# A float32 matmul with leaky ReLU: the transposes of A on VectorE as 32-bit elements, with stationary operands interleaved by two

One core of one Trainium2 chip. The metric is the time on the device in microseconds (us), the median of several executions; lower is better.

## The reference

```python
def setup_inputs():
    m, k, n = 4096, 4096, 4096
    return {"a": randn(m, k) float32, "b": randn(k, n) float32, "alpha": 0.01}     # shortened

def reference(a, b, alpha):
    x = np.matmul(a, b)
    return np.where(x > 0, x, alpha * x)
```

## The kernel before

The kernel rounds both inputs to bf16 while it loads them and keeps TensorE busy with 8192 matmuls of 128x128 by 128x512. It hands A to its matmuls with k on the partitions, so A has to be transposed. The first block (512 rows by 1024 in k) goes through TensorE itself ("turned"); all the others are loaded by GpSimd's queue into `a16` and transposed by VectorE in 32x32 squares, 62 instructions in all, each for 256 rows and 1024 in k.

```python
KC, NT, MT, NP = 8, 512, 4, 2           # KC: neighbours in k that share a partition
...
at[mb, h, u] = at_pool.tile([P, KC, RM], BF16, name="at")          # stationary operands

def load_a(mb, h, u, mp):
    dst = new_a(mb, h, u)[:, :, 2 * mp * P:2 * (mp + 1) * P]
    ...                                                             # 4 loads into a16
    nc.vector.transpose(
        dst.rearrange("p c (g i) -> p g c i", g=8), a16.rearrange("p g (j c) -> p g c j", c=KC)
    )

def mm(ps, mb, h, pi, u, mt, nt, c, first, last):
    nc.tensor.matmul(ps, at[mb, h, u][:, c, mt * P:(mt + 1) * P],
                     bt[pi, u][:, c, nt * NT:(nt + 1) * NT], start=first, stop=last)

def quarter_of(pieces, quarter):        # spreads the loads of a later step over this one
    for piece in pieces[len(pieces) * quarter // 4:len(pieces) * (quarter + 1) // 4]:
        piece()

# the first rows and columns go in eight steps of 64 matmuls; a step that ends a turn adds its
# PSUM banks into SBUF, one of four blocks of rows at a time:
for quarter in range(4):
    ...                                 # 16 matmuls
    if last:
        spill(t, h, quarter, banks)     # two VectorE adds
    quarter_of(following, quarter)      # loads and transposes for the step after
```

With two pieces, `quarter_of` places them at the end of the second and of the fourth quarter of a step, so the last transpose for the next step stands behind the last adds of this one. And inside a 32x32 square the transpose reads elements that lie KC = 8 bf16 values, 16 bytes, apart.

Of the kernel before, what the change touches and what calls it, by code (L numbers as in the profile page):

```python
# [8 lines left out]
P = 128  # L9
BF16 = mybir.dt.bfloat16  # L10
FP32 = mybir.dt.float32
LRELU = mybir.ActivationFunctionType.Lrelu
KC = 8
NT = 512
# [9 lines left out]
def kernel(  # L24
# [4 lines left out]
    alpha,  # L29
    out: bass.AP,  # L30
):



# [8 lines left out]
    nc = tc.nc  # L43
# [7 lines left out]
    RM = MT * P  # L51
# [8 lines left out]
    at_pool = ctx.enter_context(tc.tile_pool(name="at", bufs=HALVES * KU))  # L60
# [12 lines left out]
    w = small_pool.tile([P, NT], BF16, name="w")  # L73
    nc.vector.memset(w, 0.0)  # L74
    x = small_pool.tile([P, 8], FP32, name="x")
    nc.vector.memset(x, 0.0)  # L76
    nc.scalar.activation(x, x, LRELU, alpha=alpha)  # L77
    wp = psum_pool.tile([P, NT], FP32, name="ps")
    for _ in range(8):
        nc.tensor.matmul(wp, w[:, :P], w, start=True, stop=True)  # L80

    at = {}
    bt = {}

    def new_a(mb, h, u):
        if (mb, h, u) not in at:
            at[mb, h, u] = at_pool.tile([P, KC, RM], BF16, name="at")
        return at[mb, h, u]

    def new_b(pi, u):  # L90
# [3 lines left out]

    def load_a(mb, h, u, mp):

        dst = new_a(mb, h, u)[:, :, 2 * mp * P:2 * (mp + 1) * P]
        row = (mb * HALVES + h) * RM + 2 * mp * P
        a16 = a16_pool.tile([P, 8, QW], BF16, name="a16")
        for q in range(4):  # L100
            src = a[row:row + 2 * P, u * KW + q * QW:u * KW + (q + 1) * QW]
            nc.gpsimd.dma_start(a16[32 * q:32 * q + 32], src.rearrange("(g i) w -> i g w", i=32))  # L102
        nc.vector.transpose(  # L103
            dst.rearrange("p c (g i) -> p g c i", g=8), a16.rearrange("p g (j c) -> p g c j", c=KC)
        )

    def b_rows(n, u, c):
# [7 lines left out]
    def mm(ps, mb, h, pi, u, mt, nt, c, first, last):  # L115
        nc.tensor.matmul(  # L116
            ps,
            at[mb, h, u][:, c, mt * P:(mt + 1) * P],
            bt[pi, u][:, c, nt * NT:(nt + 1) * NT],
            start=first,  # L120
            stop=last,
        )

    def new_banks():
        return {
            (mt, nt): psum_pool.tile([P, NT], FP32, name="ps")
            for mt in range(MT)
# [3 lines left out]
    def place(mb, h, n, mt):  # L131
        row = ((mb * HALVES + h) * MT + mt) * P
        return out[row:row + P, n * RN:(n + 1) * RN]
# [20 lines left out]
    for mb in range(1, MB):  # L154
        first = next(i for i, r in enumerate(regions) if r[0] == mb)
        for h in range(HALVES):
            for u in range(KU):
                loads.setdefault(first * KU + h * KU + u - 2 * KU + 1, []).extend(
                    lambda mb=mb, h=h, u=u, mp=mp: load_a(mb, h, u, mp) for mp in range(MT // 2)
                )  # L160
# [13 lines left out]
    def step_loads(h, u):  # L174
        if h:
            return [lambda mp=mp: load_a(0, 1, u, mp) for mp in range(MT // 2)]
        made = [lambda c=c: load_b(0, pairs[0], u, c) for c in range(KC)]
        made.insert(4, lambda: load_a(0, 0, u, 1))
        made.insert(0, lambda: load_a(0, 0, u, 0))
        return made  # L180
# [4 lines left out]
    def spill(t, h, mt, banks):  # L185
# [10 lines left out]
        if t == len(TURNS) - 1:  # L196
            o = o_pool.tile([P, RN], FP32, name="o")
            nc.scalar.activation(o, part[h][:, mt, :], LRELU, alpha=alpha)  # L198
            nc.scalar.dma_start(place(0, h, pairs[0], mt), o)


    a_in = bt_pool.tile([P, MT, KW], FP32, name="a_in", tag="bt")
    b_in = [part_pool.tile([P, KC // 2, RN], FP32, name="b_in", tag="part") for _ in range(2)]
    a_rounded = at_pool.tile([P, MT, KW], BF16, name="a_rounded", tag="at")
    order = [("a", 0), ("b", 0), ("a", 1), ("b", 1), ("b", 2), ("a", 2), ("b", 3), ("a", 3),
             ("b", 4), ("b", 5), ("b", 6), ("b", 7)]
    for what, i in order:
        if what == "a":
            nc.sync.dma_start(a_in[:, i, :], a[i * P:(i + 1) * P, :KW])  # L209
        else:  # L210
            nc.sync.dma_start(b_in[i // 4][:, i % 4, :], b_rows(pairs[0], 0, i))  # L211
    a0 = new_a(0, 0, 0)
    b0 = new_b(0, 0)
    turned = {
        (mt, i): psum_pool.tile([P, KC // 2, P], BF16, name="turned", tag="ps")
        for mt in range(MT)
        for i in range(2)
    }
    banks = new_banks()

    def take(what, i):
        if what == "b":
            nc.scalar.copy(b0[:, i, :], b_in[i // 4][:, i % 4, :])  # L223
            return
        nc.vector.tensor_copy(a_rounded[:, i, :], a_in[:, i, :])  # L225
        cols = a_rounded[:, i, :].rearrange("m (p c) -> m c p", c=KC)
        for c in range(KC):
            nc.tensor.transpose(turned[i, c // 4][:, c % 4, :], cols[:, c, :], ident)  # L228
        nc.scalar.copy(a0[:, :4, i * P:(i + 1) * P], turned[i, 0])  # L229
        nc.vector.tensor_copy(a0[:, 4:, i * P:(i + 1) * P], turned[i, 1])  # L230

    there = {"a": [], "b": []}
    ready = []
# [1 line left out]
    for n, (what, i) in enumerate(order):  # L235
        take(what, i)
        if (what, i) == ("b", 3):

            nc.gpsimd.tensor_copy(x[:, :1], b0[:, 2, :1])  # L239
        there[what].append(i)  # L240
        now = [(i, c) for c in there["b"]] if what == "a" else [(mt, i) for mt in there["a"]]
        ready.append(now)
        for mt, c in ready[n - 1] if n else []:
            for nt in range(NP):
                mm(banks[mt, nt], 0, 0, 0, 0, mt, nt, c, (mt, nt) not in begun, False)
                begun.add((mt, nt))
# [3 lines left out]
    for mt, c in ready[-1]:  # L250
        for nt in range(NP):
            mm(banks[mt, nt], 0, 0, 0, 0, mt, nt, c, False, True)
        spill(0, 0, mt, banks)
# [3 lines left out]
    for i in range(1, len(steps)):  # L257
        t, h, u, first, last = steps[i]
        following = queue[i + 1] if 2 <= i and i + 1 < len(steps) else []
        own = 2 * KU - 2 + i - (len(steps) - 2)  # L260
        if first:
            banks = new_banks()
            if h not in part:
                part[h] = part_pool.tile([P, MT, RN], FP32, name="part", tag="part")
        for quarter in range(4):
            if last:
                todo = [(quarter, c) for c in range(KC)]
            else:
                todo = [(mt, c) for c in (2 * quarter, 2 * quarter + 1) for mt in range(MT)]
            for mt, c in todo:  # L270
                for nt in range(NP):
                    mm(banks[mt, nt], 0, h, 0, u, mt, nt, c, first and c == 0,
                       last and c == KC - 1)
            if last:
                spill(t, h, quarter, banks)
            quarter_of(following, quarter)
            if own >= 2 * KU - 2:
                quarter_of(loads.get(own, []), quarter)


    for r in range(HALVES, len(regions)):
        mb, h, pi, n = regions[r]
        banks = new_banks()
        final = r == len(regions) - 1
        for u in range(KU):
            last = u == KU - 1
            for mt in range(MT):
# [7 lines left out]
                if last:  # L295
                    o = o_pool.tile([P, RN], FP32, name="o")
                    to = place(mb, h, n, mt)
                    for nt in range(NP):
                        cols = slice(nt * NT, (nt + 1) * NT)
                        nc.scalar.activation(o[:, cols], banks[mt, nt], LRELU, alpha=alpha)  # L300
                        if final:
# [39 lines left out]
```

## Time and profile before

| kernel before | value | where from |
|---|---|---|
| time | 1795.21 us (1794.66 to 1795.24) | three executions |
| pace of matmuls | 215.8 ns | chain of waits, after 110 us |
| gaps of TensorE after 20 us | 6.36 us, four | waits |
| half clock after the largest gap | about 6.8 us | windows |
| one transpose on VectorE | 3842 ns | groups |
| VectorE busy | 264.3 us | page, part 1 |

In the lines PE is TensorE, PEld its weight loads, DVE VectorE, ACT ScalarE and POOL GpSimd; L103 is line 103 of the kernel. The granted clock is the share of its full clock that TensorE got, so half clock is 0.50. A group's line ends with the idle time of the engine just before it and with what ended that. TensorE's ends are modelled, so pace is read from starts. In a line of the windows the columns are: stretch, its length, busy us (and instructions) of TensorE, of its weight loads, of VectorE, ScalarE and GpSimd, then granted clock, busy share of the DMA engines and GB/s. The prediction shows the lines themselves.

### The profile page before, as it was taken

The numbers are of one execution on the slowest core, as the hardware profiler recorded it, in microseconds if no ns is written. First come the engines' busy times: TensorE is split into PE (matmuls) and PEld (weight loads), VectorE is DVE, ScalarE is ACT, GpSimd is POOL, SyncE is SP. The second block draws the span as 40 slices with busy tenths as digits, with TensorE's granted clock in tenths as the row PEclk, the third lists the DMA queues.
The fourth block names the chain that finished last, engine by engine and source line by source line (L and its number), as shares of the span: only waits on it lengthen the run. The fifth ranks groups of instructions, "written<-read, shape, count | busy, mean of one in ns | idle before, by whom it ended". The sixth has DMA issues, their size and how long they took to land.

```text
span 1794.5 us, 17965 instructions
## 1 busy us (share of the span) xinstructions
PE 1771.5 (99%) x8068; PEld 806.3 (45%) x8232; DVE 264.3 (15%) x112; ACT 155.1 (9%) x270; POOL 360.7 (20%) x663
## 2 busy tenths in 40 slices
PE   8999999999999999999999999999999999999999
PEld 4434444444444444444444444444444444444444
DVE  5750000055300000005520000000551000000000
ACT  3010000000000000000000000000000000000001
POOL 4530110333002021033300202004320120201000
PEclk9999999999999999999999999999999999999999
DMA  9993571987319256298713916539770481835511
GB/s 253 195 239 86 122 160 47 182 127 123 85 58 194 55 118 141 63 200 124 122 56 88 192 48 117 119 94 197 125 124 24 101 180 48 157 78 117 118 47 47
DMA packets 147020, 214.06 MB, mean 119 GB/s; under 512 B 12800, under 2 KB 76288, under 8 KB 146944
## 3 DMA queue, kind: packets, MB, share of 16 engines
q0 software_dynamic: 126208, 139.50, 48.1%
q10 hardware_dynamic: 17856, 65.02, 9.3%
q1 hardware_dynamic: 2880, 8.39, 1.2%
q8 instruction: 64, 1.05, 0.2%
q14 instruction: 12, 0.10, 0.0%
HBM read 285.21 MB, written 67.11 MB: 196 GB/s over the span
## 4 chain that ended last, share of the span: by engine, by line
PE 97%; DMA 2%; issue 1%; DVE 0%; ACT 0%; POOL 0%; SPq 0%; DVEq 0%; POOLq 0%
PE ps L116 97%; DMA a<-in_a_dram 1%; DMA a_in<-in_a_dram 0%; DVE at L103 0%; DVE part L195 0%; PE turned L228 0%; ACT part L193 0%; POOL a L102 0%; DVE a_rounded L225 0%; ACT o L300 0%; SPq L211 0%; SPq L209 0%; DVEq L195 0%; POOLq L102 0%
## 5 line engine op out<-in xcount | busy, mean ns | idle before, releaser
L116 PE MATMUL ps<-bt,at 128*128 128x512 bf16 x8028 | 1765.0, 380 | 14.9 <-DVE at L103 5.5
L116 PEld LDWEIGHTS <-at 128*128 128x128 bf16 x8192 | 802.3, 98 | 976.1 <-DVE at L103 7.4
L113 POOL DMA_DIRECT2D bt<-in_b_dram x408 | 217.3, 539 | 1097.4 <-PE ps L116 908.0
L103 DVE STREAM_TRANSPOSE at<-a 128x2048 bf16<-128x2048 bf16 x62 | 235.6, 3842 | 1046.0 <-PE ps L116 1033.7
L300 ACT ACTIVATE o<-ps 128x512 f32<-128x512 f32 x240 | 130.7, 595 | 1524.6 <-PE ps L116 1462.5
L102 POOL DMA_DIRECT2D a<-in_a_dram x248 | 142.3, 579 | 201.3 <-DVE at L103 142.8
L195 DVE TENSOR_TENSOR part<-ps,part 128x512 f32<-128x512 f32 x32 | 20.3, 680 | 33.7 <-PE ps L116 31.6
L198 ACT ACTIVATE o<-part 128x1024 f32<-128x1024 f32 x8 | 8.5, 1057 | 86.0 <-DVE part L195 79.2
L223 ACT CAST bt<-b_in 128x1024 bf16<-128x1024 f32 x8 | 8.1, 1045 | 2.2 <-DMA b_in<-in_b_dram 2.0
L228 PE MATMUL turned<-ident,a_rounded 128*128 128x128 bf16 x32 | 3.6, 276 | 3.3 <-DVE a_rounded L225 3.3
L193 ACT COPY part<-ps 128x512 f32<-128x512 f32 x8 | 4.4, 594 | 14.2 <-PE ps L116 14.2
L228 PEld LDWEIGHTS <-a_rounded 128*128 128x128 bf16 x32 | 3.1, 156 | 5.2 <-DVE a_rounded L225 4.7
L191 DVE COPY part<-ps 128x512 f32<-128x512 f32 x8 | 5.2, 838 | 0.0
L80 PE MATMUL ps<-w 128*128 128x512 bf16 x8 | 3.6, 631 | 1.2 <-DVE x L76 1.2
L225 DVE CAST a_rounded<-a_in 128x1024 bf16<-128x1024 f32 x4 | 2.8, 693 | 6.5 <-DMA a_in<-in_a_dram 6.5
L229 ACT COPY at<-turned 128x512 bf16<-128x512 bf16 x4 | 2.3, 585 | 8.6 <-PE turned L228 8.6
L239 POOL CAST x<-bt 128x1 f32<-128x1 bf16 x1 | 0.6, 558 | 11.1 <-ACT bt L223 11.1
L230 DVE COPY at<-turned 128x512 bf16<-128x512 bf16 x4 | 1.7, 424 | 5.2 <-PE turned L228 5.2
L80 PEld LDWEIGHTS <-w 128*128 128x128 bf16 x8 | 1.0, 142 | 2.8 <-issue 1.6
L77 ACT ACT_TABLE_LOAD x1 | 1.3, 1283 | 0.7 <-PEq L322 0.7
L74 DVE MEMSET w<- 128x256 uint32 x1 | 0.3, 272 | 0.9 <-PEq L322 0.9
masks.py:199 POOL TENSOR_SCALAR_AFFINE_SELECT ident<-ident 128x128 bf16<-128x128 bf16 x1 | 0.3, 287 | 0.1
(7 smaller groups left out, 0.9 us busy)
## 6 DMA issues: line engine op xcount, KB each, us to landing
bt<-in_b_dram POOLq DMA_DIRECT2D x408, 256.0 KB, 7.6
out_dram<-o ACTq DMA_DIRECT2D x124, 512.0 KB, 3.8
a<-in_a_dram POOLq DMA_DIRECT2D x248, 128.0 KB, 5.0
b_in<-in_b_dram SPq DMA_DIRECT2D x8, 512.0 KB, 9.6
a_in<-in_a_dram SPq DMA_DIRECT2D x4, 512.0 KB, 7.8
out_dram<-o SPq DMA_DIRECT2D x8, 256.0 KB, 2.0
```

The source lines that it names most:

```text
L80: nc.tensor.matmul(wp, w[:, :P], w, start=True, stop=True)
L102: nc.gpsimd.dma_start(a16[32 * q:32 * q + 32], src.rearrange("(g i) w -> i g w", i=32))
L103: nc.vector.transpose(dst.rearrange("p c (g i) -> p g c i", g=8), a16.rearrange("p g (j c) -> p g c j", c=KC))
L113: nc.gpsimd.dma_start(new_b(pi, u)[:, c, :], b_rows(n, u, c))
L116: nc.tensor.matmul(ps, at[mb, h, u][:, c, mt * P:(mt + 1) * P], bt[pi, u][:, c, nt * NT:(nt + 1) * NT], start=first, stop=last,)
L191: nc.vector.tensor_copy(kept, banks[mt, nt])
L193: nc.scalar.copy(kept, banks[mt, nt])
L195: nc.vector.tensor_add(kept, banks[mt, nt], kept)
L198: nc.scalar.activation(o, part[h][:, mt, :], LRELU, alpha=alpha)
L223: nc.scalar.copy(b0[:, i, :], b_in[i // 4][:, i % 4, :])
L228: nc.tensor.transpose(turned[i, c // 4][:, c % 4, :], cols[:, c, :], ident)
L300: nc.scalar.activation(o[:, cols], banks[mt, nt], LRELU, alpha=alpha)
```

## The change

VectorE is to transpose half as many elements: two bf16 neighbours in k count as one 32-bit element. A square of 32x32 such elements then carries two columns of k at once, so the stationary operands of two neighbours lie interleaved, and TensorE reads its 128 columns 4 bytes apart.

```diff
-at[mb, h, u] = at_pool.tile([P, KC, RM], BF16, name="at")
+at[mb, h, u] = at_pool.tile([P, KC // 2, RM, 2], BF16, name="at")
...
         nc.vector.transpose(
-            dst.rearrange("p c (g i) -> p g c i", g=8), a16.rearrange("p g (j c) -> p g c j", c=KC)
+            dst.rearrange("p c m e -> p c (m e)").bitcast(U32).rearrange("p c (g i) -> p g c i", g=8),
+            a16.rearrange("p g w -> p (g w)").bitcast(U32)
+            .rearrange("p (g j c) -> p g c j", g=8, c=KC // 2),
         )
...
-            at[mb, h, u][:, c, mt * P:(mt + 1) * P],
+            at[mb, h, u][:, c // 2, mt * P:(mt + 1) * P, c % 2],
...
-        nc.scalar.copy(a0[:, :4, i * P:(i + 1) * P], turned[i, 0])
-        nc.vector.tensor_copy(a0[:, 4:, i * P:(i + 1) * P], turned[i, 1])
+        for half, copy in ((0, nc.scalar.copy), (1, nc.vector.tensor_copy)):
+            copy(
+                a0[:, 2 * half:2 * half + 2, i * P:(i + 1) * P, :].rearrange("p c m e -> p c e m"),
+                turned[i, half].rearrange("p (c e) m -> p c e m", e=2),
+            )
```

The read step stays 16 bytes: four 32-bit elements in place of eight of 16 bits.

## The prediction

> **What bounds the kernel now.** I read the page first, for the engine that fills the span.

> ```profile
> span 1794.5 us, 17965 instructions
> PE 1771.5 (99%) x8068; PEld 806.3 (45%) x8232; DVE 264.3 (15%) x112; ACT 155.1 (9%) x270; POOL 360.7 (20%) x663
> L116 PE MATMUL ps<-bt,at 128*128 128x512 bf16 x8028 | 1765.0, 380 | 14.9 <-DVE at L103 5.5
> L116 PEld LDWEIGHTS <-at 128*128 128x128 bf16 x8192 | 802.3, 98 | 976.1 <-DVE at L103 7.4
> L103 DVE STREAM_TRANSPOSE at<-a 128x2048 bf16<-128x2048 bf16 x62 | 235.6, 3842 | 1046.0 <-PE ps L116 1033.7
> L230 DVE COPY at<-turned 128x512 bf16<-128x512 bf16 x4 | 1.7, 424 | 5.2 <-PE turned L228 5.2
> ```

> TensorE is busy all the time; VectorE, whose work the change halves, is busy for 15% of it. A matmul's 380 ns is a modelled, overlapping duration. The pace is in the chain in order of time: its pieces of 49 recorded matmuls start 10.79 us apart, which is 50 matmuls (2% of the records, 164 of 8192, are missing) and 215.8 ns each. 8192 x 215.8 ns = 1767.8 us. So at most 1794.5 - 1767.8 = 26.7 us are not steady matmuls, and the change can gain from those alone. About 10 us of them pass before the first real matmul. The rest is in the waits and the TensorE timeline:

> ```profile
> DVE at L103 <- PE ps L116: 1033.7, 23, 337.7
> POOL a L102 <- DVE at L103: 142.8, 32, 7.8
> DVE at L103 <- DMA a<-in_a_dram: 6.0, 1, 6.0
> PE ps L116 <- DVE at L103: 5.5, 2, 4.0
> PE ps L116 <- ACT part L193: 0.6, 1, 0.6
> PE ps L116 <- DVE part L195: 0.2, 1, 0.2
> ```

> ```profile
> 27.39 42.48 PE L116 MATMUL ps<-bt,at 128*128 128x512 bf16 x193 [0.60 <-ACT part L193]
> 71.40 0.73 PE L116 MATMUL ps<-bt,at 128*128 128x512 bf16 x2 [1.54 <-DVE at L103]
> 72.35 27.14 PE L116 MATMUL ps<-bt,at 128*128 128x512 bf16 x123 [0.22 <-DVE part L195]
> 103.50 26.78 PE L116 MATMUL ps<-bt,at 128*128 128x512 bf16 x108 [4.00 <-DVE at L103]
> ```

> Four gaps, 6.36 us, all before 104 us. After 110 us TensorE waits for no other engine. There VectorE waits 1033.7 us for TensorE, and what waits for VectorE is the issue of loads needed much later. The chain charges 1.3% to loads of A; I don't believe it, since VectorE waited for such a load only once (6.0 us, before the first transpose). The largest gap, seen from VectorE, and what follows it, in windows (PE, weight loads, DVE, ACT, POOL, then the granted clock):

> ```profile
> 98.45 1.29 DVE L195 TENSOR_TENSOR part<-ps,part 128x512 f32<-128x512 f32 x2 [0.65 <-PE ps L116]
> 99.66 11.19 DVE L103 STREAM_TRANSPOSE at<-a 128x2048 bf16<-128x2048 bf16 x3
> 102.00:103.00 1.00, 0.00 (x0) 0.00 (x0) 1.00 (x1) 0.00 (x0) 0.38 (x1) 0.75 1.12 281
> 106.00:107.00 1.00, 1.00 (x4) 0.42 (x3) 1.00 (x1) 0.00 (x0) 0.23 (x1) 0.50 1.06 307
> 110.00:111.00 1.00, 1.00 (x6) 0.49 (x5) 0.84 (x1) 0.00 (x0) 0.24 (x2) 1.00 1.14 213
> ```

> The transpose of the second half of the next A block stands in program order behind the last add of the step before, so it cannot start until TensorE has ended that step. TensorE then does four matmuls and sits idle for the rest of the transpose. The clock drops to 0.50 at about 102.5, 3.0 us into the gap, and returns at about 109.2. In between weight loads start 427 ns apart: 5.7 us / 0.427 = 13.5 matmuls, each 211 ns late, 2.85 us more. The gap costs nearly 7 us, not 4.

> [...]

> **The change part by part.** No instruction is added or removed: each engine has as many, in the same order; only patterns and widths differ.

> *Transposes (62).* Each handles 1024 elements of four bytes in place of 2048 of two. Elements on the reading side still lie 16 bytes apart. A 32x32 block takes 3842/64 = 60 ns now[...]. If that stays per element, the new duration is half, 1.92 us; I take 1.95.[...] VectorE loses 62 x 1.89 = 117 us of busy time, 264 to about 147, and that by itself is worth nothing.

> *Gap at 103.50.* It ends with a transpose that starts at 99.74 and takes 3.71 us here; 1.9 us off leaves about 2.1 us: -1.9 us.[...] I give 3 in 4 that the clock stays up: -2.85 x 0.75 = -2.1 us.

> *Gaps at 71.40 and 72.35.* The transpose at 67.31 follows an add that ends when TensorE still has about 2.4 us of the step to go. With 1.95 us, also removing the lateness inherited from the transposes at 56.28 and 61.20, it ends near 68.7, before TensorE asks for it at about 69.7; the next add then starts sooner as well. Some 0.1 us may stay: -1.6 us.

> *Gap at 27.39.* ScalarE's copy and the first transpose (23.37 to about 27.2) end together. If the copy only came last by chance, 0.6 goes; if it rules, nothing: -0.3 us.

> *Start.* The four VectorE copies out of PSUM now write at a step of two elements[...]. ScalarE's four (585 ns)[...] stay. Only the copy ahead of the last cast of A stands close to TensorE's path (0.05 us of slack before the last transposes at 16.20): +0.3 us.

> *Weight loads (8192).* This is the one part on the path everywhere. Columns lie 4 bytes apart, not 2. The kernel contains a harsher test: the 32 loads of the first transposes step by 16 bytes. The last eight of them, with the clock up, took 142 to 152 ns against 98, and eight load-and-transpose pairs went by in 0.66 us. A 4-byte step should lie between: I expect 98 to 125 ns. Under a matmul's 215.8 ns even 150 stays hidden. 0 us.

> Sum: 1795.2 - 1.9 - 2.1 - 1.6 - 0.3 + 0.3 = 1789.6, say **1789.5 us**, a third of a per cent.

> **The rivals.** *A: strided weight loads slow the stream.* For: each is before its matmul, all 8192 count, and one nanosecond on the pace is 8.2 us, more than the whole gain. Against: 117 ns of slack and the 16-byte loads. If the pace took 4.5 ns more the kernel would be 2% slower, about 1830 us. I give any visible slowing 6%. *B: a four-byte transpose costs twice a two-byte one* (limited by bytes or by two passes). Then all gaps stay and the start costs 0.3: 1795.5 us.[...] 10%. *C: the transpose drops to 1.2 us* because single two-byte writes were the limit: 0.7 us more from the large gap, and the clock surely stays up: 1788 us. 25%. *D: the clock still falls* after a 2.1 us gap: 1791.7 us. *E: a load takes the place of the transpose.* Early on the DMA engines are always busy (9 in the first slices), and a faster VectorE could find A not there. Against: issues land in 7 us (median), and the loads for the critical transposes were issued over 15 us ahead; only the first transpose had to wait. It would keep 1 to 2 us of the gain.

> **Range and chances.** Removing every gap and the clock drop gives 1795.2 - 6.4 - 2.85 = 1786, the low end. The high end, 1795, covers B nearly, D and E. Beyond 2% faster there is nothing to win (26.7 us of 1794.5 is 1.5%); beyond 2% slower only A. Faster 0.01, same 0.96, slower 0.03.

> **What would show it.** Right: transposes near 1.95 us, VectorE busy near 147 us; the gap near 100 us at about 2 us with the clock at 1.00 after it; no gap over 0.4 us near 70;[...] weight loads under 150 ns and chain pieces still 10.79 us apart. Wrong: another spacing of those pieces (A), transposes at 3.8 us (B), a clock of 0.5 after the gap (D), or a TensorE or VectorE wait for a load of A near 70 or 100 us (E).

## The result

1789.38 us, the median of four executions (1787.44 to 1790.58), against 1794.93 us before. The ratio is 0.997, with a 95% interval of 0.9952 to 0.9987. It is a small gain, "same" at the 2% line. Five more executions beside the experiments gave 1787.88 us (1787.49 to 1790.3), ratio 0.9962. The changed kernel spreads over 3 us; why is part of what follows.

The page of the changed kernel, with the lines that answer to those shown of before:

```profile
span 1785.7 us, 18129 instructions
PE 1775.6 (99%) x8232; PEld 805.0 (45%) x8232; DVE 153.8 (9%) x112; ACT 155.5 (9%) x270; POOL 360.9 (20%) x663
L120 PE MATMUL ps<-bt,at 128*128 128x512 bf16 x8192 | 1769.8, 379 | 2.2 <-DVE at L105 2.2
L120 PEld LDWEIGHTS <-at 128*128 128x128 bf16 x8192 | 801.6, 98 | 969.1 <-DVE at L105 2.7
L105 DVE STREAM_TRANSPOSE at<-a 128x1024 uint32<-128x1024 uint32 x62 | 123.0, 2020 | 1136.0 <-PE ps L120 1123.6
L234 ACT COPY at<-turned 128x512 bf16<-128x512 bf16 x4 | 2.9, 730 | 7.2 <-PE turned L232 7.2
L234 DVE COPY at<-turned 128x512 bf16<-128x512 bf16 x4 | 2.9, 733 | 3.7 <-PE turned L232 3.7
```

The transpose fell from 3842 to 2020 ns. The weight loads, now at a 4-byte step, take 98 ns as before. The copies from PSUM at the start became slower on both engines, 733 ns for 424 on VectorE and 730 for 585 on ScalarE. TensorE waits 2.2 us for VectorE's transposes, and for nothing else, after the start. Its timeline has a single gap (the number in brackets is the idle time):

```profile
15.31 80.02 PE L120 MATMUL ps<-bt,at 128*128 128x512 bf16 x370
97.55 42.69 PE L120 MATMUL ps<-bt,at 128*128 128x512 bf16 x197 [2.22 <-DVE at L105]
```

Of the four gaps before, those at 27.39, 71.40 and 72.35 us are gone, and that of 4.00 us is 2.22 us. From the windows of the same run, one in the gap and one after it:

```profile
96.00:97.00 1.00, 0.00 (x0) 0.00 (x0) 1.00 (x1) 0.62 (x1) 0.54 (x1) 1.00 1.44 193
98.00:99.00 1.00, 1.00 (x6) 0.49 (x5) 1.00 (x1) 0.00 (x0) 0.80 (x2) 1.00 1.17 280
```

The last but two number is the granted clock: it stays at 1.00, where the kernel before had 0.50 after its gap. For the pace, the chain in order of time from 300 to 600 us, first a piece of the kernel before (one record in fifty is missing there), then the whole of it in the changed kernel:

```profile
306.44 10.74 PE ps L116 x49
317.24 10.74 PE ps L116 x49
```

```profile
299.96 300.22 PE ps L120 x1391
```

10.79 us for 50 matmuls and 300.22 us for 1391 are both 215.8 ns.

The two profiled spans differ by 8.8 us, and the parts add up to that: gaps 6.36 - 2.22 = 4.1 us; 0.5 us more for the three gaps that vanished, since each began at a modelled end, 0.16 us later than the pace (379 - 216 ns); half clock 2.85 us; and a start of the steady matmuls at 15.31 in place of 16.70 us, 1.4 us. The last item isn't credited to the change: this start differs from execution to execution (below). The profiled execution of the changed kernel was the fastest of its four, that of the kernel before, 1796.25 us, lay above all its four timed ones. Over many executions the gain is 5 to 7 us.

### The profile page after: what moved, and what is told of

It reads as the page before. It is cut to its first block, busy times and chain, and to the rows that moved or that the text cites. A ratio compares the mean times of both kernels' runs of the same rounds, so it can differ in the third digit from the quotient of the medians.

```text
span 1785.7 us, 18129 instructions
## 1 busy us (share of the span) xinstructions
PE 1775.6 (99%) x8232; PEld 805.0 (45%) x8232; DVE 153.8 (9%) x112; ACT 155.5 (9%) x270; POOL 360.9 (20%) x663
## 4 chain that ended last, share of the span: by engine, by line
PE 99%; DMA 0%; DVE 0%; SPq 0%; issue 0%; ACT 0%; DVEq 0%
PE ps L120 99%; DMA a_in<-in_a_dram 0%; DVE at L105 0%; SPq L215 0%; PE turned L232 0%; SPq L213 0%; DVE part L199 0%; DVE a_rounded L229 0%; ACT o L307 0%; DVEq L105 0%
## 5 line engine op out<-in xcount | busy, mean ns | idle before, releaser
L105 DVE STREAM_TRANSPOSE at<-a 128x1024 uint32<-128x1024 uint32 x62 | 123.0, 2020 | 1136.0 <-PE ps L120 1123.6
L195 DVE COPY part<-ps 128x512 f32<-128x512 f32 x8 | 5.0, 691 | 0.2 <-PE ps L120 0.2
```

Of the source, the lines that this page charges most:

```text
L105: nc.vector.transpose(dst.rearrange("p c m e -> p c (m e)").bitcast(U32).rearrange("p c (g i) -> p g c i", g=8), a16.rearrange("p g w -> p ...
L195: nc.vector.tensor_copy(kept, banks[mt, nt])
```

## The experiments

The theory: the gain is what a shorter transpose saves at a few places before 105 us, together with the clock, which fell to 0.50 with the gap of 4.00 us. The rivals: the layout or the start brings it; VectorE's time or traffic over the whole run counts; strided weight loads cost something; loads take the transposes' place. The line numbers differ between kernels; the names of the tiles don't.

### The changed kernel again

No edit.

> The changed kernel once more, for more samples and a second profile. Theory (the gain is the shorter transposes in the gaps before 105 us, and the clock that does not fall): about 5 to 6 us below the kernel before, the gap near 97 us at 2.2 us, no gap near 70 us. The first four timed runs lay 3.1 us apart, and the profiled one was the fastest and started its steady matmuls 1.4 us earlier than the kernel before. Rival (the clock falls in some executions after a 2.2 us gap): a run of 1790 us or more with a stretch at half clock after the gap. If the spread is only in the start, the clock stays at 1.00 after 20 us.

1787.88 us against 1795.19. The gap is again 2.22 us, yet in this execution the clock did fall:

```profile
98.00:99.00 1.00, 0.91 (x3) 0.36 (x4) 1.00 (x2) 0.00 (x0) 0.78 (x2) 0.71 1.16 209
100.00:101.00 1.00, 1.00 (x4) 0.38 (x3) 1.00 (x1) 0.00 (x0) 0.02 (x1) 0.50 1.07 307
102.00:103.00 1.00, 1.00 (x6) 0.44 (x5) 0.00 (x0) 0.00 (x0) 0.12 (x1) 1.00 1.07 303
```

The half clock lasted from about 98.4 to 101.8 us, 3.4 us, half as long as in the kernel before, and cost 1.7 us. So the prediction's rival D occurs in some executions. The profiles hold six gaps of 2.2 us (this one, the first profile's, and those of "first rows", "forms", the first try of the layout alone, and "every transpose twice" near 70 us, all below); the clock fell after three of them, this one and the last and "forms", each time for 3.4 us.

The falls of the clock explain part of the 3 us of spread. The start is another part: the steady matmuls began between 14.9 and 17.1 us over the profiles of all versions but that with the 16-byte step, and the later the half clock of the start ended (10.8 to 14.8 us in the ten traces of these that record its end), the later they began (correlation 0.90; which of the two is the cause was not tested). The gapless version below spreads over 1.8 us in ten executions.

### The transposes one quarter earlier

```diff
-for piece in pieces[len(pieces) * quarter // 4:len(pieces) * (quarter + 1) // 4]:
+for piece in pieces[(len(pieces) * quarter + 3) // 4:(len(pieces) * (quarter + 1) + 3) // 4]:
```

With two pieces this places them at the end of the first and third quarters. On the changed kernel:

> The changed kernel with the first rows' transposes of A one quarter of a step earlier in program order, so that the transpose no longer stands behind the last adds of a step. Theory: the 2.2 us gap goes, 2 us below the changed kernel, about 1787 us, and the clock never falls after the start. Rival (the gap is really the load of A landing late): the gap stays, now put down to a load.

1785.47 us (1785.26 to 1785.66), ratio 0.9944 to the kernel before; again on another chip, 1785.22 us, ratio 0.9947. What was expected there:

> The changed kernel with the earlier transposes, as the partner of the run above on the same chip, and to see on another day or chip that it holds: 1785 to 1786 us, no gap after 20 us.

TensorE's timeline has no gap at all:

```profile
15.73 124.48 PE L120 MATMUL ps<-bt,at 128*128 128x512 bf16 x576
```

In the first of these runs the spread fell to 0.4 us too. On the kernel before, with its two-byte transposes and plain layout:

> The kernel before (two-byte transposes, plain layout) with the same earlier place in program order. Theory: the 3.84 us transpose fits between the third block's adds and the end of the step, so the 4.0 us gap and the clock drop after it go (6.9 us) and part of the gaps near 70 us; about 1787 to 1789 us, as good as the changed kernel, with slow transposes. Rival (the width of the transposes itself is what counts, by less traffic or less VectorE time over the whole run): it stays near 1795 us.

1789.08 us (1788.49 to 1790.47), ratio 0.9966, with transposes of 3842 ns:

```profile
69.75 0.94 PE L116 MATMUL ps<-bt,at 128*128 128x512 bf16 x3 [0.65 <-DVE at L103]
70.92 27.14 PE L116 MATMUL ps<-bt,at 128*128 128x512 bf16 x125 [0.22 <-DVE part L195]
98.68 0.94 PE L116 MATMUL ps<-bt,at 128*128 128x512 bf16 x3 [0.62 <-DVE at L103]
99.84 40.52 PE L116 MATMUL ps<-bt,at 128*128 128x512 bf16 x187 [0.22 <-DVE part L195]
```

The gap of 4.00 us shrank to 0.62 + 0.22 us and the clock stayed up. One line of scheduling brings about as much as the whole change, and the two together more than either, since a long transpose still makes VectorE late by some 0.6 us near 70 and 98 us. What counts is when a transpose ends, not how wide its elements are.

### Four-byte transposes for the first rows only

```diff
+        if mb:
+            nc.vector.transpose(...)      # as in the kernel before, plain layout
+            return
```

> Four-byte transposes and the interleaved layout only for the first 1024 rows of A (14 of the 62 transposes); the other 48 as before. Theory: only those before 105 us are on the path, so the time equals that of the changed kernel within 1 us, and VectorE is busy about 48 x 1.82 = 87 us longer than there. Rival (VectorE's time over the whole run counts, or strided weight loads cost something later): it differs from the changed kernel by over 2 us.

1790.24 us (1788.02 to 1790.39), ratio 0.997 against the changed kernel's 0.9962 in the same rounds. The medians lie 2.4 us apart, more than I expected and by itself over the rival's 2 us, but the executions of both reach from about 1788 to 1790.4, and the medians mostly say where more of them fell; by the means (1789.6 and 1788.6) it is 1.0 us. The trace has the same single gap, 2.21 us, and the rest of the run is without any. VectorE is busy for 241.3 us against 153.6, 88 us more, and that cost TensorE no wait. The 48 later transposes are off the path.

### The layout alone, twice

The first try wrote the new layout by two two-byte transposes, for the even and then for the odd columns:

```diff
+        for e in range(2):                # second try: for e in (1, 0)
+            nc.vector.transpose(
+                dst[:, :, :, e].rearrange("p c (g i) -> p g c i", g=8), src16[:, :, :, e, :]
+            )
```

> The interleaved layout alone: two-byte transposes write it, in two instructions of 1024 elements each (even and odd columns). Theory: the pair takes about 3.9 us, all gaps and the clock drop are as in the kernel before, the pace of the matmuls stays 215.8 ns; 1795 us, plus up to 0.3 us at the start. Rival (the layout or its strided weight loads brings or costs time): differs from the kernel before by over 2 us.

1793.1 us (1790.04 to 1794.96), ratio 0.999 (0.9977 to 1.0002). Not what I had in mind: TensorE uses an even column first, so it went on after the first half, and the large gap in the trace was 2.23 us. The second try turned the order round:

> The interleaved layout alone once more, because the first try had a flaw: its two half transposes wrote the even columns first, which TensorE uses first, so the gap near 100 us was only 2.2 us. Here the odd columns come first, so that TensorE has to wait for both halves, about 4 us. Theory: gaps and clock drop as in the kernel before, pace 215.8 ns, time within 1.5 us of the kernel before. Rival (the layout itself brings the gain of the first try, 1.8 us or more): again 1793 us or less.

1795.48 us, ratio 1.0005 (0.9992 to 1.0017), with the gap back:

```profile
101.99 38.23 PE L120 MATMUL ps<-bt,at 128*128 128x512 bf16 x163 [4.11 <-DVE at L107]
```

The half clock is back as well (0.60 from 100 to 105 us), and the pace from 300 to 600 us is again 1391 matmuls in 300.22 us. The layout gains and costs nothing that can be measured. The first try shows in passing that splitting a transpose, so that what is needed first ends first, halves the gap too.

### Every transpose twice, and one of them twice

```diff
-        nc.vector.transpose(...)
+        for _ in range(2):                # the other: range(2 if (mb, h, u, mp) == (0, 1, 2, 1) else 1)
+            nc.vector.transpose(...)
```

> The changed kernel with every four-byte transpose done twice in a row, 2 x 2.02 us, so as long as the old one. Theory: the gain is undone, gap of 4.2 us near 97 to 100 us, half clock after it, gaps near 70 us back; 1794 to 1796 us. Rival (width or traffic counts, not the duration at that place): stays near 1789 us.

1797.34 us against 1794.87, ratio 1.0011 (0.9998 to 1.0025). The gain is undone (whether more than that is lost is within the interval): gaps of 0.27 us near 26, 2.24 us near 70 and 4.23 us near 104 us, and here the clock fell after both of the long ones.

> The changed kernel with one single transpose of 62 done twice: the one that stands in the 2.2 us gap. Theory: the gap grows by 2.0 us to 4.2 us, the clock falls to half for some 5.7 us after it and costs another 2.85 us: 4.9 us above the changed kernel. Rival (the gap costs only itself, the clock has another reason): 2.0 us above it.

1793.28 us, ratio 0.9988 (0.9976 to 1.0001), where the changed kernel had 0.9962 beside the kernel before of another chip: 0.26% or 4.7 us more for one instruction of 2.0 us, as expected. Each of the two ratios is uncertain by about 2 us, so the times alone don't exclude the rival's 2.0 us; the trace does. Timeline and windows of this kernel:

```profile
101.12 39.23 PE L121 MATMUL ps<-bt,at 128*128 128x512 bf16 x165 [4.23 <-DVE at L106]
```

```profile
100.00:101.00 1.00, 0.00 (x0) 0.00 (x0) 1.00 (x2) 0.00 (x0) 0.62 (x2) 0.50 1.09 313
104.00:106.00 2.00, 2.00 (x6) 0.76 (x5) 0.85 (x1) 0.00 (x0) 0.54 (x1) 0.50 1.12 260
106.00:108.00 2.00, 2.00 (x8) 0.79 (x7) 0.00 (x0) 0.00 (x0) 0.54 (x2) 0.80 1.12 209
```

The gap grew by 2.0 us, and the clock was at half from 100.0 to 106.8 us, where the two profiles of the changed kernel had none and 3.4 us of it. A gap costs itself and then, if enough of it falls into one period (2.14 us or more of 3.41 in all 12 cases above), the clock.

### Forms of the transpose

```diff
+            nc.vector.transpose(n16(o16, 1), n16(i16, 1))    # and so on, in VectorE's idle time
```

Eleven extra instructions on a scratch tile, to see whether the 16-byte step between reads sets a transpose's duration, or the transposing itself.

> The changed kernel with eleven extra VectorE instructions on a scratch tile, while VectorE is idle for 300 us; wanted is the duration of each form, not the time. Read step in elements: two-byte transposes of 2048 elements at 1, 2, 4, 8, then written at 2; four-byte ones of 1024 elements at 1, 2, 4, 8; half of one. If the 16-byte step between reads[...], the two-byte transpose at step 1 takes about 2.2 us, at step 8 3.84, and the four-byte one at step 1 1.2 us. If the transposing itself does, all two-byte forms take 3.84 us and all four-byte ones 2.02. The whole should stay within 2 us of the changed kernel.

Groups by form. In the order of the fence: two-byte elements read at a step of 2, 8 and 16 bytes, then read at 2 and written at 4; four-byte ones read at 4, 8, 16 and 32 bytes.

```profile
L298 DVE STREAM_TRANSPOSE scratch<-scratch 128x2048 bf16<-128x2048 bf16 x1 | 2.3, 2311 | 0.0
...
L300 DVE STREAM_TRANSPOSE scratch<-scratch 128x2048 bf16<-128x2048 bf16 x1 | 2.3, 2311 | 0.0
L301 DVE STREAM_TRANSPOSE scratch<-scratch 128x2048 bf16<-128x2048 bf16 x1 | 3.9, 3882 | 0.0
L302 DVE STREAM_TRANSPOSE scratch<-scratch 128x2048 bf16<-128x2048 bf16 x1 | 2.5, 2479 | 0.0
L303 DVE STREAM_TRANSPOSE scratch<-scratch 128x1024 uint32<-128x1024 uint32 x1 | 1.2, 1247 | 0.0
L304 DVE STREAM_TRANSPOSE scratch<-scratch 128x1024 uint32<-128x1024 uint32 x1 | 1.2, 1247 | 0.0
L305 DVE STREAM_TRANSPOSE scratch<-scratch 128x1024 uint32<-128x1024 uint32 x1 | 2.0, 2019 | 0.0
L306 DVE STREAM_TRANSPOSE scratch<-scratch 128x1024 uint32<-128x1024 uint32 x1 | 2.0, 2041 | 0.0
```

It is the read step. At 2 to 8 bytes 2048 two-byte elements take 2311 ns and, at 4 and 8 bytes, 1024 four-byte ones 1247 ns; at 16 bytes they take 3882 and 2019 ns, and a step of 32 bytes costs hardly more than one of 16 (2041 and 2019 ns). From the differences I estimate 1.04 ns an element up to 8 bytes, whatever its width ((2311 - 1247) / 1024), and 1.82 ns at 16 bytes ((3882 - 2019) / 1024), 1.75 times as much. Why the cost rises between 8 and 16 bytes was not shown. A two-byte transpose at an 8-byte step took 2311 ns on the scratch tile, little more than the new one's 2020. The whole program took 1789.77 us in its one execution.

### Weight loads at a 16-byte step

```diff
-            at[mb, h, u] = at_pool.tile([P, KC, RM], BF16, name="at")
+            at[mb, h, u] = at_pool.tile([P, RM, KC], BF16, name="at")
...
-            at[mb, h, u][:, c, mt * P:(mt + 1) * P],
+            at[mb, h, u][:, mt * P:(mt + 1) * P, c],
```

On the kernel before, with the writers changed to match.

> The weight loads' rival taken to an extreme: the kernel before with all eight columns interleaved, so that the 128 columns of a stationary operand lie 16 bytes apart, written by two-byte transposes. Theory: a weight load takes 140 to 150 ns in place of 98, still hidden under a matmul, whose pace stays at 215.8 ns after 110 us; the time is that of the kernel before, plus what slower transposes (writing at 16 bytes) add to the gaps before 105 us. Rival (a strided weight load slows the stream of matmuls): the pace after 110 us rises, and each ns of it shows as 7.6 us.

1845.86 us, ratio 1.028. The page and, below, the chain from 300 to 600 us:

```profile
L116 PEld LDWEIGHTS <-at 128*128 128x128 bf16 x8192 | 1175.2, 144 | 653.9 <-DVE at L103 47.9
L103 DVE STREAM_TRANSPOSE at<-a 128x2048 bf16<-128x2048 bf16 x62 | 580.9, 9726 | 818.9 <-PE ps L116 817.9
```

```profile
300.00 300.01 PE ps L116 x1390
```

A weight load takes 144 ns in place of 98, and the pace stays 215.8 ns: strided weight loads are hidden, even at four times the step of the change. I had not foreseen the size of the rest. Two-byte elements written 16 bytes apart make the transpose 9726 ns long, in place of 3842, and a copy of 512 elements from PSUM 2445 ns on either engine, in place of 424 on VectorE and 585 on ScalarE. TensorE waits 38.3 us for the transposes; the clock falls repeatedly (0.987 on average over the run). That is why the kernel is slower, not the weight loads.

### The copies at the start

```diff
-            at[mb, h, u] = at_pool.tile([P, KC // 2, RM, 2], BF16, name="at")
+            at[mb, h, u] = at_pool.tile(
+                [P, KC // 2, RM, 2] if mb or h or u else [P, KC, RM], BF16, name="at")
```

With the matching copies and matmuls, on the version without gaps.

> The version without any gap, with the plain layout for the very first A block alone, so that the eight PSUM copies at the start run at 424 ns (VectorE) and 585 ns (ScalarE) in place of 733 and 730. The prediction charged +0.3 us for them. Theory: 0 to 0.5 us faster than the version without gaps run beside it. Rival (in the profiles the changed kernels reach steady matmuls 0.6 to 1.4 us earlier than the kernel before, so the interleaved copies would help): slower than it by 0.5 us or more.

1786.05 us (1784.86 to 1786.76) against 1785.22 (1784.96 to 1786.79) beside it; ratios 0.9951 and 0.9947, whose intervals overlap widely. The copies do take 585 and 425 ns again, but what they cost or save is within the spread of the start: in the profiles the steady matmuls began at 15.12 us with the fast copies and at 17.06 and 15.73 us with the slow ones, and the layout alone had 15.07 us without being faster than the kernel before. Undecided, and under 1 us either way.

## Why the prediction was right

The time, 1789.5 us predicted and 1789.38 measured, agrees better than its terms deserve. Point by point:

- **Where the gain can be.** Right. "First rows" shows that only the first 14 transposes count, and "one twice" that a single one of them is worth 4.7 us.
- **Transpose 1.95 us.** Measured 2.02; VectorE was busy for 153.8 us where 147 were expected. The argument "if that stays per element" held, and "forms" gives its reason, the 16-byte read step, which I had noted as unchanged without knowing it to be the limit. The 1.2 us of rival C is what "forms" shows at a step of 4 or 8 bytes (1247 ns).
- **Gap at 103.50, about 2.1 us left.** Measured 2.22. It is still the transpose behind the last adds: with the transpose earlier, it is gone.
- **Clock, 3 in 4 that it stays up.** Too hopeful: it fell after three of six gaps of this length. The odds were my estimate. A period with a third busy (2.22 us idle of 3.41, in "after again") was followed by half clock, and the three gaps that the clock outlasted had a border inside (1.81 + 0.42 us at the most uneven). With a border every 3.41 us, at a random place, and a limit between 1.81 and 2.14 us, I estimate 40 to 60% for a fall. When the clock falls, it costs 1.7 us, not 2.85. The expected value, half of 1.7 lost, is close to the 0.75 us that I had set aside, by luck.
- **Gaps at 71.40 and 72.35, 1.6 us.** Both gone, and worth a little more, since idle time counted from modelled ends is 0.16 us short for each gap.
- **Gap at 27.39, 0.3 us.** Gone whole, although ScalarE's copies begin 8.62 us after the steady matmuls as before (23.93 - 15.31 and 25.32 - 16.70), so the transpose ruled there and the copy only came last by chance. It is gone in the kernel before with the earlier place too, where the first transpose began 0.5 us sooner after the steady matmuls (6.16 us for 6.67).
- **Start, +0.3 us.** The charge was my estimate. VectorE's copies take 733 ns, from 424, and ScalarE's 730, where I had said they would stay at 585. The 0.05 us of slack was misread: it is issue time in the chain. The last cast ended at 15.42 us and the weight load that needs it began at 15.99 us without waiting, so 0.57 us were free, more than the 0.31 us by which the copy before it grew. The cost itself could not be shown.
- **Weight loads, 0 us.** Right: 98 ns, and the pace did not move. Rival A fell, at four times the step too.
- **Rival E, loads in the transposes' place.** VectorE now waits for loads of A four times, 12.4 us, before once for 6.0. One of them, 1.76 us before the transpose at 71.73 us, is a sign that the prediction had named for E, but none of these waits reached TensorE.

## What to carry to other kernels

When an engine that is 15% busy is made twice as fast, count the places where another engine waits for it; here one transpose behind the last adds of a step held most of the gain (4.7 of 5 to 7 us), and a change of one line in the program order of the first rows' transposes was worth as much as halving all 62. Rate a gap in TensorE with the half clock that can follow it: 4 us cost 7, and the same gap of 2.2 us cost 2.2 or 3.9, by where the clock's period happened to lie. Before widening elements, look at the bytes between reads: 2048 two-byte elements took 2311 ns at 8 bytes and 3882 at 16.
